# State update as a sum and a scaling, with transposes by the transpose operation, in a two-layer RWKV-7 and GLA backbone

## The chip, the core and the metric

The kernel runs on one core of a Trainium2 chip. The time is the device time of one execution in microseconds (us); of several runs the median is given. A core has five engines that run their own instruction streams and wait for each other by semaphores: TensorE (PE, with its weight loads shown as PEld), VectorE (DVE), ScalarE (ACT), GpSimd (POOL) and SyncE (SP, which issues the DMAs here).

## The reference, cut to what matters

Two layers over 512 latent and 256 context tokens of width 1024. Each has a token mixer (an input projection, an RWKV-7 branch and a GLA branch, both in two directions, gates, an output projection) and an MLP of width 4096, with normalisation and modulation around both. The change touches the recurrent states of the two branches:

```python
def rwkv7_scan(r, decay, k, v, kk, a, s0, reverse):
    def step(s, inp):
        r_t, w_t, k_t, v_t, kk_t, a_t = inp
        sa = jnp.einsum("bhvk,bhk->bhv", s, kk_t)
        s = (s * w_t[:, :, None, :]
             - sa[..., None] * (kk_t * a_t)[:, :, None, :]
             + v_t[..., None] * k_t[:, :, None, :])
        return s, jnp.einsum("bhvk,bhk->bhv", s, r_t)

def gla_chunked(q, k, v, log_alpha, s0):   # chunks of 64
    ...
    def step(s, inp):
        dec, kv = inp
        return s * dec[..., None] + kv, s
```

## The kernel before, in words

Activations are held with channels on the partitions and tokens along the free dimension. Large products (tiles `d`, from activations `sh`, `sl` and weights `wh`, `wl`) are made of three fp32r products of high and low parts; products of the recurrences are plain fp32 and take two passes on PE each.

The RWKV recurrence is done in chunks of 64 tokens. A unit is a pair of heads (p, 4 of them) and a group (gi, 3 of them: the context, then two halves of the latents) in both directions, so a layer has 12 RWKV units; 6 GLA units follow. For a unit, `rw_A1` and `rw_A2` make decays and scaled keys, `rw_B` makes masked products, transposes them (`pe.transpose`, tile `TK`) and inverts a triangular matrix, and `rw_C` walks four steps (chunks) in order. One step of `rw_C` (line 1335) multiplies the state `ZS` into `c` (line 1345), copies it to `pre` by ACT and DVE, multiplies by the inverse `YI`, copies to `ZA`, and updates the state: the product of `TK` and `ZA` (line 1364) is scaled by the chunk's decay `E` and added to the old state, which ACT has scaled by `E` into `zse` (line 1342). Per step that is four ACT copies and four DVE operations of 64x64, one for each of two directions and two heads (halves of the partitions). The last step of the last group needs no update, so a pair has 11 updating steps and a layer 44.

`gla_C` does the same with states `GZ` of 64x128 and the scaled copies `ze` (lines 1603 to 1609); its products `c<-GZ,KT` read only parts of `GZ` that are not the state, and are made for two steps at once. A layer has 22 such steps.

Row vectors on partitions become broadcast tiles by a product with the identity: `rstd_b` (line 812, tile `sc`), `sum_sq` (line 842, `rn`), the modulation vectors `da<-C,acc` (lines 764 and 1964). `C` holds the identity.

The order of the work is set by class `Order`. It records every instruction, gives each a price (`add`, line 209), and places them engine by engine in a list schedule: among those that can start first, the one of least `prio`, that is its place in the program, later by `LATE` for dense products (line 560). It issues them at one line, 566, which every row of the profile therefore has. Neighbouring PE products of one kind make one piece of the schedule (line 277). The mixer's program order comes from weaving threads per unit window: `nfill` and `nada` (line 103) say how many gate column blocks and modulation pieces each window gets, and `SEG` (line 142) gives the schedule's settings for the five flushed segments: the start, mixer, MLP, mixer, MLP.

Of the kernel before, what the change touches and what calls it, by code (L numbers as in the profile page):

```python
# [53 lines left out]
def constants():  # L54
# [45 lines left out]
SB = 6  # L100

CFG = {
    "nfill": ((2, 2, 0, 3, 1, 0, 3, 1, 0, 2, 2, 0, 2, 1, 1, 0, 0, 0, 0), (2, 3, 0, 2, 2, 1, 2, 2, 0, 2, 0, 0, 2, 1, 1, 0, 0, 0, 0)),
    "nada": ((2, 2, 2, 2, 2, 2, 2, 2, 2, 1, 2, 2, 0, 1, 0, 0, 0, 0, 0), (2, 1, 3, 1, 3, 2, 3, 1, 0, 0, 0, 0, 0, 0, 0, 0, 0, 0, 0)),
# [37 lines left out]
SEG = [  # L142
    dict(AHEAD=20.0, HOLD=8000.0, HYST=0.0, LATE=80000.0, LATEF=80000.0, SLACK=0.0, WARM=0.45),
    dict(AHEAD=100.0, HOLD=1000000000.0, HYST=0.0, LATE=20000.0, LATEF=20000.0, SLACK=0.0, WARM=0.45),
    dict(AHEAD=20.0, HOLD=1000000000.0, HYST=0.0, LATE=20000.0, LATEF=20000.0, SLACK=0.0, WARM=0.45),
    dict(AHEAD=20.0, HOLD=8000.0, HYST=0.0, LATE=20000.0, LATEF=20000.0, SLACK=0.0, WARM=0.45),
    dict(AHEAD=20.0, HOLD=1000000000.0, HYST=0.0, LATE=20000.0, LATEF=20000.0, SLACK=0.0, WARM=0.6),
]


class Order:
# [57 lines left out]
    def add(self, key, op, fn, a, k):  # L209
# [36 lines left out]
        else:  # L246
            c = max(w(out), max([w(x) for x in ins if x.ap and len(x.ap) > 1], default=0))
            onchip = [x for x in ins if hasattr(x.tensor, "cap_key")]
            if key == "ACT":
                n["d"] = 175.0 + 0.87 * c + (100.0 if any(isinstance(k.get(x), bass.AP) for x in ("bias", "scale")) and c > 64 else 0.0)  # L250
                n["table"] = 1 if k.get("func") == AF.Ln else 0 if k.get("func") in (AF.Exp, AF.Tanh) else None
            elif key == "POOL":
                if op == "memset":
                    n["d"] = 90.0 + 0.85 * c
                elif op in ("tensor_copy", "tensor_scalar"):
                    n["d"] = 180.0 + 0.87 * c
                elif k.get("op") == ALU.pow:
                    n["d"] = 380.0 + 160.0 * c
                else:
                    n["d"] = 185.0 + 2.16 * c  # L260
                n["two"] = op == "tensor_tensor"
            else:
# [6 lines left out]
                else:  # L269
                    n["d"] = 150.0 + 1.05 * c  # L270
        if key == "PE":
# [5 lines left out]
            if GROUP and p is not None and p.get("kind") == n["kind"] and p["calls"] < (3 if lhs.dtype == F32R else 4 if n["dense"] else 16):  # L277
# [51 lines left out]
    def flush(self):  # L329
# [6 lines left out]
        for n in ns:  # L336
# [6 lines left out]
            for name, t in ts.items():  # L343
                left[name] = left.get(name, 0) + 1
                if name not in self.serial:
                    key = t.cap_key
                    kk = self.slots.setdefault(key, {"cap": t.bufs or t.tag_meta.bufs, "free": [], "used": 0, "next": {}, "n": {}, "t0": self.free0})
                    sub = "da" if name.startswith("da_") else ""
# [225 lines left out]
def hybrid_kernel(ctx: ExitStack, tc: tile.TileContext, A: dict, out: bass.AP):  # L574
# [171 lines left out]
    def ada_steps(l, b0, pl, tag, bufs):  # L746
# [16 lines left out]
        for s in range(4):  # L763
            mm(pt[:, s].rearrange("p g r -> p (g r)"), acc[:, 128 * s:128 * s + 128], ident)
# [43 lines left out]
    def rstd_b(rb, streams, ps_pool, use):  # L808
        for s, o, n in streams:
            b = ps_pool.tile([P, 512], F32, name="d", tag="d")  # L810
            for t in range(o // 128, (o + n) // 128):
                mm(b[:, 128 * t - o:128 * t - o + 128], rb[:, 128 * t:128 * t + 128], ident)
            use(s, o, n, b[:, 0:n])

    def sum_sq(pl, xs, grp, cuts, eng=pool, psp=ops):
# [25 lines left out]
        for t in range(nt):  # L841
            mm(b[:, 128 * t:128 * t + 128], rn[:, t:t + 1].to_broadcast([P, 128]), ident)
# [81 lines left out]
    def mixer(l, acts, adas, pre, early):  # L924
# [399 lines left out]
        def rw_C(X, gi):  # L1324
# [10 lines left out]
            for st in range(4):  # L1335
                cc = (st, 7 - st)
                sl = slice(st, 8 - st, 7 - 2 * st)
                if not (gi == NG - 1 and st == 3):
                    zse = G([P, 2, 64], "zse", 1)
                    for d in range(2):  # L1340
                        for h in range(2):
                            act.activation(out=zse[HS[h], d], in_=zs[HS[h], cc[d], h, :], func=AF.Copy, scale=E[HS[h], cc[d]:cc[d] + 1])
# [15 lines left out]
                if st < 3:  # L1358
                    nz, ns = zs, (st + 1, 6 - st)
                else:  # L1360
                    nz, ns = nzs, (0, 7)
# [217 lines left out]
        def gla_C(X, gi):  # L1579
# [9 lines left out]
            for st in range(4):  # L1589
# [11 lines left out]
                cc = (st, 7 - st)  # L1601
                nz, ns = (z, (st + 1, 6 - st)) if st < 3 else (nz_, (0, 7))
                ze = G([P, 2, 128], "Q", 2, name="ze")
                for d in range(2):
# [470 lines left out]
```

## Time and profile before

| | us |
|---|---|
| median of 3 runs | 2871.23 |
| lowest and highest | 2870.66, 2878.29 |
| profiled execution | 2886.5 |
| its span | 2884.7 |
| PE busy | 2714.0 (94%) |
| DVE busy | 1603.8 (56%) |
| ACT busy | 1470.5 (51%) |
| POOL busy | 1172.0 (41%) |
| mean granted clock of PE | 0.967 |

The profile is of one execution, so its parts add up to its own 2886.5 us. PE's rows overlap each other, since a product's latency is counted with it: what a product takes is read from one start to the next. Tiles are named by the program; a row like `c<-ZA,TK` is an instruction that writes a tile `c` and reads `ZA` and `TK`.

### The profile page before, as it was taken

The numbers are of one execution on the slowest core, as the hardware profiler recorded it, in microseconds if no ns is written. First come the engines' busy times: TensorE is split into PE (matmuls) and PEld (weight loads), VectorE is DVE, ScalarE is ACT, GpSimd is POOL, SyncE is SP. The second block draws the span as 40 slices with busy tenths as digits, with TensorE's granted clock in tenths as the row PEclk, the third lists the DMA queues.
The fourth block names the chain that finished last, engine by engine and source line by source line (L and its number), as shares of the span: only waits on it lengthen the run. The fifth ranks groups of instructions, "written<-read, shape, count | busy, mean of one in ns | idle before, by whom it ended". The sixth has DMA issues, their size and how long they took to land.

```text
span 2884.7 us, 57083 instructions
## 1 busy us (share of the span) xinstructions
PE 2714.0 (94%) x22596; PEld 2249.0 (78%) x22596; DVE 1603.8 (56%) x3154; ACT 1470.5 (51%) x3144; POOL 1172.0 (41%) x1336
## 2 busy tenths in 40 slices
PE   7999999999989989999999899989988988999998
PEld 6777877788767878888888666767776766888887
DVE  6677787775576351122224547787877677622224
ACT  4565655666773452313134545656566785633333
POOL 3653444443321642313135546434434232733335
PEclk9999999999999999999998999999988999999999
DMA  6322333222226322222223342223211125433334
GB/s 232 110 85 73 97 95 97 84 90 65 87 94 229 94 77 63 64 64 64 63 70 116 119 143 87 77 85 90 92 34 35 34 77 182 136 106 97 97 95 136
DMA packets 148444, 276.59 MB, mean 96 GB/s; under 512 B 16496, under 2 KB 25456, under 8 KB 148176
## 3 DMA queue, kind: packets, MB, share of 16 engines
q1 hardware_dynamic: 148176, 272.93, 30.4%
q8 instruction: 178, 2.92, 0.4%
q14 instruction: 90, 0.74, 0.1%
HBM read 242.85 MB, written 30.02 MB: 95 GB/s over the span
## 4 chain that ended last, share of the span: by engine, by line
PE 51%; DVE 7%; ACT 4%; POOL 4%; issue 2%; DMA 1%; SPq 0%; POOLq 0%; ACTq 0%; DVEq 0%
PE d L566 43%; PE c L566 3%; PE m L566 2%; PE i L566 2%; POOL wl L566 1%; POOL S L566 1%; POOL x L566 1%; DVE sl L566 1%; DVE ZS L566 1%; DVE AR L566 1%; DVE u L566 1%; ACT zse L566 1%; PE da L566 1%; DVE GZ L566 0%; ACT f L566 0%
## 5 line engine op out<-in xcount | busy, mean ns | idle before, releaser
L566 PE MATMUL d<-sh,wh 128*128 128x512 f32 (+1 forms) x3280 | 1199.2, 366 | 39.0 <-ACT sh L566 13.2
L566 PE MATMUL d<-sh,wl 128*128 128x512 f32 (+1 forms) x3280 | 1142.4, 348 | 19.1 <-POOL wl L566 16.4
L566 PE MATMUL d<-sl,wh 128*128 128x512 f32 (+1 forms) x3280 | 1142.1, 348 | 4.4 <-DVE sl L566 3.0
L566 POOL TENSOR_TENSOR wl<-wr,wh 128x512 fp32r<-128x512 f32 x356 | 476.0, 1339 | 793.9 <-ACT wh L566 770.6
L566 PEld LDWEIGHTS d<-sh,wh 128*128 128x128 f32 x3280 | 631.3, 192 | 150.0 <-issue 36.5
L566 PEld LDWEIGHTS d<-sh,wl 128*128 128x128 f32 x3280 | 631.0, 192 | 103.8 <-POOL wl L566 21.9
L566 PEld LDWEIGHTS d<-sl,wh 128*128 128x128 f32 x3280 | 632.7, 193 | 69.0 <-DVE sl L566 5.4
L566 ACT ACTIVATE wh<-wr 128x512 fp32r<-128x512 f32 x580 | 361.9, 627 | 469.3 <-PE d L566 389.6
L566 DVE TENSOR_TENSOR wl<-wr,wh 128x512 fp32r<-128x512 f32 x224 | 171.5, 770 | 187.0 <-ACT wh L566 178.9
L566 DVE TENSOR_TENSOR t<-t,d 128x512 f32<-128x512 f32 (+1 forms) x101 | 58.2, 576 | 318.2 <-ACT t L566 318.1
L566 POOL TENSOR_TENSOR sl<-t,sh 128x512 fp32r<-128x512 f32 (+2 forms) x72 | 103.3, 1435 | 204.8 <-ACT sh L566 204.7
L566 DVE TENSOR_TENSOR a<-a,d 128x512 f32<-128x512 f32 (+1 forms) x80 | 44.3, 554 | 232.7 <-PE d L566 232.7
L566 ACT ACTIVATE zse<-ZS,E 64x64 f32<-64x64 f32 x352 | 121.3, 345 | 67.2 <-DVE ZS L566 62.7
L566 ACT ACTIVATE XY<-i 128x512 f16<-128x512 f32 x192 | 107.8, 591 | 59.1 <-PE i L566 57.1
L566 ACT ACTIVATE t<-d 128x512 f32<-128x512 f32 (+1 forms) x101 | 51.4, 509 | 161.4 <-PE d L566 161.3
L566 DVE SCALAR_TENSOR_TENSOR ZS<-c,E,zse 64x64 f32<-64x64 f32 x352 | 99.5, 283 | 34.6 <-PE c L566 27.6
L566 POOL TENSOR_TENSOR LTL<-AB,LTB 64x512 f16<-64x512 f32 x48 | 63.9, 1332 | 122.1 <-DVE LTB L566 88.1
L566 POOL TENSOR_TENSOR rn<-rn,C 128x2 f32<-128x2 f32 (+2 forms) x41 | 59.3, 1446 | 101.4 <-DVE rn L566 94.9
L566 POOL TENSOR_TENSOR S<-S,q 128x256 f32<-128x256 f32 x92 | 76.5, 838 | 56.5 <-ACT q L566 52.8
L566 PEld LDWEIGHTS <-XY 64*64 64x64 f16 x1920 | 65.7, 110 | 38.9 <-issue 27.2
L566 DVE TENSOR_TENSOR Q<-i,MK 128x512 f16<-128x512 f32 x120 | 82.7, 689 | 23.3 <-PE i L566 20.7
L566 ACT ACTIVATE f<-d 128x512 f32<-128x512 f32 (+1 forms) x85 | 54.0, 644 | 79.1 <-PE d L566 69.2
(255 smaller groups left out, 4309.6 us busy)
## 6 DMA issues: line engine op xcount, KB each, us to landing
wr<-in_w_dram SPq DMA_DIRECT2D x304, 256.0 KB, 2.6
wr<-in_win_dram SPq DMA_DIRECT2D x180, 256.0 KB, 2.9
wa<-in_ada_dram SPq DMA_DIRECT2D x160, 256.0 KB, 2.7
wr<-in_wmrg_dram SPq DMA_DIRECT2D x64, 256.0 KB, 2.9
ra<-in_ada_dram SPq DMA_DIRECT2D x32, 256.0 KB, 5.4
wr<-in_wout_dram SPq DMA_DIRECT2D x32, 256.0 KB, 3.0
gdr<-fg SPq DMA_DIRECT2D x20, 384.0 KB, 2.9
gdr<-fg SPq DMA_DIRECT2D x20, 256.0 KB, 2.3
```

What stands on the lines that cost most here:

```text
L566: ins = fn(*a, **k).ins
```

## The change

The state update becomes one sum and one scaling: (product + old state) times decay. In layer one the sum is a DVE addition into a scratch tile `gs` with one buffer, then a DVE multiplication by `E` broadcast along the free dimension; both take the two directions in one operation, so there are two additions and two multiplications of 64x128 per step. In layer two (`ACCUM`) PE adds the old state in PSUM by a product of the identity with `ZS`, and only the two multiplications are left to DVE. The GLA steps of both layers use the form with the addition, at 64x256, with a scratch tile `gs2` of two buffers. The products with the identity named above become `pe.transpose`. Prices, settings and the tables of the schedule change with it.

```diff
+ACCUM = (False, True)
...
-    "nfill": ((2, 2, 0, 3, 1, 0, 3, 1, 0, 2, 2, 0, 2, 1, 1, 0, 0, 0, 0), (2, 3, 0, 2, 2, 1, 2, 2, 0, 2, 0, 0, 2, 1, 1, 0, 0, 0, 0)),
+    "nfill": ((2, 2, 0, 2, 2, 0, 2, 2, 0, 2, 2, 0, 2, 1, 1, 0, 0, 0, 0), (2, 3, 0, 2, 2, 1, 2, 2, 0, 2, 2, 0, 1, 0, 0, 1, 0, 0, 0)),
...
+SEG = [dict(LATE=1e6, LATEF=1e6), dict(LATE=20e3, LATEF=20e3), {}, {}, {}]
...
-                n["d"] = 175.0 + 0.87 * c + (100.0 if any(isinstance(k.get(x), bass.AP) for x in ("bias", "scale")) and c > 64 else 0.0)
+                n["d"] = 175.0 + 0.87 * c + (110.0 if any(isinstance(k.get(x), bass.AP) for x in ("bias", "scale")) and c > 32 else 0.0)
...
-                    n["d"] = 185.0 + 2.16 * c
+                    n["d"] = 215.0 + 2.25 * c
...
-                    n["d"] = 150.0 + 1.05 * c
+                    n["d"] = 150.0 + 1.05 * c + (60.0 if op == "scalar_tensor_tensor" and isinstance(k.get("scalar"), bass.AP) else 0.0)
...
-            mm(pt[:, s].rearrange("p g r -> p (g r)"), acc[:, 128 * s:128 * s + 128], ident)
+            pe.transpose(pt[:, s].rearrange("p g r -> p (g r)"), acc[:, 128 * s:128 * s + 128], ident)
...
-                mm(b[:, 128 * t - o:128 * t - o + 128], rb[:, 128 * t:128 * t + 128], ident)
+                pe.transpose(b[:, 128 * t - o:128 * t - o + 128], rb[:, 128 * t:128 * t + 128], ident)
...
-            mm(b[:, 128 * t:128 * t + 128], rn[:, t:t + 1].to_broadcast([P, 128]), ident)
+            pe.transpose(b[:, 128 * t:128 * t + 128], rn[:, t:t + 1].to_broadcast([P, 128]), ident)
...
-                if not (gi == NG - 1 and st == 3):
-                    zse = G([P, 2, 64], "zse", 1)
-                    for d in range(2):
-                        for h in range(2):
-                            act.activation(out=zse[HS[h], d], in_=zs[HS[h], cc[d], h, :], func=AF.Copy, scale=E[HS[h], cc[d]:cc[d] + 1])
...
                 for d in range(2):
-                    mm(fl(pr[:, d]), tk[:, cc[d]], fl(za[:, cc[d]]))
-                for d in range(2):
-                    for h in range(2):
-                        hs = HS[h]
-                        dve.scalar_tensor_tensor(out=nz[hs, ns[d], h, :], in0=pr[hs, d, h], scalar=E[hs, cc[d]:cc[d] + 1],
-                                                 in1=zse[hs, d], op0=ALU.mult, op1=ALU.add)
+                    if ACCUM[l]:
+                        mm(fl(pr[:, d]), ident, fl(zs[:, cc[d]]), stop=False)
+                    mm(fl(pr[:, d]), tk[:, cc[d]], fl(za[:, cc[d]]), start=not ACCUM[l])
+                for h in range(2):
+                    hs = HS[h]
+                    src = pr[hs, :, h]
+                    if not ACCUM[l]:
+                        src = G([P, 2, 64], "gs", 1)[hs]
+                        dve.tensor_tensor(out=src, in0=pr[hs, :, h], in1=zs[hs, sl, h, :], op=ALU.add)
+                    dve.tensor_tensor(out=nz[hs, ns, h, :], in0=src, in1=E[hs, sl].unsqueeze(2).to_broadcast([64, 2, 64]), op=ALU.mult)
...
-                ze = G([P, 2, 128], "Q", 2, name="ze")
-                for d in range(2):
-                    for h in range(2):
-                        hs = HS[h]
-                        act.activation(out=ze[hs, d], in_=z[hs, cc[d], h, :], func=AF.Copy, scale=E[hs, cc[d]:cc[d] + 1])
-                        dve.scalar_tensor_tensor(out=nz[hs, ns[d], h, :], in0=pu[hs, st % 2, d], scalar=E[hs, cc[d]:cc[d] + 1],
-                                                 in1=ze[hs, d], op0=ALU.mult, op1=ALU.add)
+                gs = G([P, 2, 128], "Q", 2, name="gs2")
+                for h in range(2):
+                    hs = HS[h]
+                    dve.tensor_tensor(out=gs[hs], in0=pu[hs, st % 2], in1=z[hs, sl, h, :], op=ALU.add)
+                    dve.tensor_tensor(out=nz[hs, ns, h, :], in0=gs[hs], in1=E[hs, sl].unsqueeze(2).to_broadcast([64, 2, 128]), op=ALU.mult)
```

`nada` becomes two pieces for each of the first 12 windows of layer one and the first 8 of layer two, with the same totals; `SEG` loses its limits on how far ahead DMAs are issued (HOLD) in the first and fourth segment.

The order that follows differs in both mixers from end to end. Three places show what the update becomes. On ACT, in a unit window of layer two, the row of `zse` stood in front of the copy `pre` before:

```order
L566 ACTIVATE XY<-i 128x512 x2
L566 ACTIVATE zse<-ZS,E 64x64 x4
L566 ACTIVATE pre<-c 64x128
L566 ACTIVATE ZS<-VT 64x4x64
L566 ACTIVATE wh<-wr 128x512
```

and now ACT has in such a place (`XY` and `Q` are of the inverse, `E`, `Ep`, `lw` decays of a later unit):

```order
L561 ACTIVATE XY<-i 128x512 x2
L561 ACTIVATE pre<-c 64x128
L561 ACTIVATE E<-lw 128x3
L561 ACTIVATE Ep<-lw,C 128x260
L561 ACTIVATE ZA<-c 64x2x64
```

Nothing that scales the state stands between the inverse's copies and `pre` any more. On PE, a step's update product in layer two, before (`LTB` is of the inverse):

```order
L566 MATMUL d<-sh,wl 128x512
L566 MATMUL c<-ZA,TK 128x128 x2
L566 MATMUL da<-wa,SC 32x128 x4
L566 MATMUL c<-ZS,AR 128x128 x2
L566 LDWEIGHTS LTB
```

and now:

```order
L561 MATMUL d<-sh,wl 128x512
L561 MATMUL c<-ZS,C 128x128
L561 MATMUL c<-ZA,TK 128x128
L561 MATMUL c<-ZS,C 128x128
L561 MATMUL c<-ZA,TK 128x128
L561 LDWEIGHTS LTB
```

One product with the identity stands before the first product that reads `ZA`, the other behind it. On DVE, in the GLA windows of layer two, before:

```order
L566 SCALAR_TENSOR_TENSOR GZ<-c,E,ze 64x128 x4
L566 SCALAR_TENSOR_TENSOR sc<-f,PR,sc 128x769 x2
L566 SCALAR_TENSOR_TENSOR GZ<-c,E,ze 64x128 x4
L566 TENSOR_TENSOR sl<-bon,sh 128x512
L566 SCALAR_TENSOR_TENSOR GZ<-c,E,ze 64x128 x4
```

and now, each multiplication reading what the addition in front of it wrote:

```order
L561 TENSOR_TENSOR gs_20341<-c,GZ 64x256
L561 TENSOR_TENSOR GZ<-gs_20341,E 64x2x128
L561 TENSOR_TENSOR gs_20341<-c,GZ 64x256
L561 TENSOR_TENSOR GZ<-gs_20341,E 64x2x128
L561 SCALAR_TENSOR_TENSOR y<-y,PR,d 128x512
```

Where four independent operations stood, two dependent pairs stand.

## Rows read from the trace of the kernel before

**Rows 1.** The page: the span, and the granted clock in 40 slices (tenths)

```profile
span 2884.7 us, 57083 instructions
...
PEclk9999999999999999999998999999988999999999
...
```

**Rows 2.** Windows: length, busy us and count of PE, PEld, DVE, ACT, POOL; clock, DMA

```profile
...
124.00:719.00 595.00, 583.24 (x6867) 473.96 (x6868) 440.21 (x936) 356.25 (x838) 259.25 (x334) 1.00 0.28 85
719.00:873.00 154.00, 139.68 (x1144) 112.24 (x1138) 103.91 (x220) 111.89 (x227) 39.27 (x58) 0.96 0.28 90
1029.00:1550.00 521.00, 517.88 (x2918) 451.83 (x2917) 116.90 (x199) 157.21 (x281) 162.06 (x123) 1.00 0.23 68
1746.00:2270.00 524.00, 483.14 (x5646) 383.57 (x5644) 405.01 (x854) 322.41 (x771) 227.50 (x289) 0.93 0.23 68
2270.00:2410.00 140.00, 116.89 (x912) 90.42 (x911) 100.24 (x201) 107.39 (x222) 35.81 (x60) 0.93 0.22 68
...
```

**Rows 3.** Chain of waits, shares of the windows 1746:2270 and 2270:2410

```profile
...
by line: PE d L566 26.9%; PE c L566 17.4%; PE i L566 8.8%; PE m L566 8.3%; DVE ZS L566 3.7%; issue 3.5%; ACT zse L566 3.3%; DVE AR L566 3.0%; PE da L566 2.7%; DVE ZA L566 2.0%; DVE AB L566 1.8%; DVE YI L566 1.1%; DVE Q L566 1.0%; DVE pre L5
...
by line: issue 20.6%; PE d L566 14.7%; DVE GZ L566 9.5%; DVE lw L566 5.8%; DVE sc L566 5.3%; ACT L566 4.6%; DVE QS L566 4.4%; PE m L566 4.2%; ACT ta L566 3.4%; PE c L566 3.3%; ACT ze L566 2.8%; ACT GZ L566 2.4%; ACT f L566 2.1%; ACT sc L566
...
```

**Rows 4.** Timeline, one step of layer two: start us, us, engine, line, operation, count [idle]

```profile
...
2123.99 1.20 DVE L566 SCALAR_TENSOR_TENSOR ZS<-c,E,zse 64x64 f32<-64x64 f32 x4
...
2124.96 0.77 PE L566 MATMUL c<-ZS,AR 128*128 128x128 f32 x4
...
2125.22 1.42 ACT L566 ACTIVATE zse<-ZS,E 64x64 f32<-64x64 f32 x4 [0.89 <-DVE ZS L566]
...
2126.66 0.27 ACT L566 ACTIVATE pre<-c 64x128 f32<-64x128 f32 x1
...
```

**Rows 5.** Groups by form: busy us, mean ns of one, idle before

```profile
...
L566 ACT ACTIVATE zse<-ZS,E 64x64 f32<-64x64 f32 x352 | 121.3, 345 | 67.2 <-DVE ZS L566 62.7
...
L566 DVE SCALAR_TENSOR_TENSOR ZS<-c,E,zse 64x64 f32<-64x64 f32 x352 | 99.5, 283 | 34.6 <-PE c L566 27.6
...
L566 ACT ACTIVATE ze<-GZ,E 64x128 f32<-64x128 f32 x176 | 70.0, 398 | 11.6 <-DVE GZ L566 7.7
...
L566 DVE SCALAR_TENSOR_TENSOR GZ<-c,E,ze 64x128 f32<-64x128 f32 x176 | 61.5, 349 | 10.6 <-PE c L566 5.1 <-ACT ze L566 0.4
...
L566 DVE TENSOR_TENSOR acc<-acc,da 128x128 f32<-128x128 f32 x140 | 39.0, 283 | 32.7 <-PE da L566 30.4
...
L566 DVE TENSOR_TENSOR BK<-ta,Ep 64x256 f32<-64x256 f32 x48 | 30.9, 644 | 1.4
...
L566 PE MATMUL d<-C,sc 128*128 128x128 f32 x176 | 26.0, 294 | 1.1 <-ACT sc L566 1.1
...
L566 DVE TENSOR_TENSOR AR<-r,lw 64x256 f32<-64x256 f32 x40 | 19.9, 498 | 0.2
...
L566 DVE TENSOR_TENSOR QS<-m,MK 64x256 f32<-64x256 f32 x40 | 16.9, 422 | 11.6 <-PE m L566 11.0
...
L566 PE MATMUL d<-C,rn 128*128 128x128 f32 x84 | 16.0, 324 | 6.0 <-DVE u L566 3.1 <-POOL rn L566 2.7
...
L566 PE MATMUL da<-C,acc 128*128 128x128 f32 x48 | 7.4, 287 | 0.8 <-ACT acc L566 0.8
...
```

**Rows 6.** Timeline of PE: four transposes, four products with the identity, the next

```profile
...
487.38 0.63 PE L566 MATMUL m<-C,BK 128*128 128x128 f32 x4
487.84 1.06 PE L566 MATMUL da<-C,acc 128*128 128x128 f32 x8
488.73 0.56 PE L566 MATMUL c<-pre,YI 128*128 128x64 f32 x4
...
```

**Rows 7.** Timeline, DVE in layer two's GLA: a dependent pair, and four updates

```profile
...
2330.54 0.42 DVE L566 TENSOR_TENSOR lw<-lw,ta 128x256 f32<-128x256 f32 x1 [4.51 <-ACT ta L566]
...
2331.06 0.70 DVE L566 TENSOR_TENSOR_SCAN lw<-C,lw 128x260 f32<-128x260 f32 x1
...
2339.00 1.50 DVE L566 SCALAR_TENSOR_TENSOR GZ<-c,E,ze 64x128 f32<-64x128 f32 x4
...
```

More of the change, by code (lines that the diff above doesn't have):

```diff
@@ L100 @@
 SB = 6
+ACCUM = (False, True)
 CFG = {
-    "nfill": ((2, 2, 0, 3, 1, 0, 3, 1, 0, 2, 2, 0, 2, 1, 1, 0, 0, 0, 0), (2, 3, 0, 2, 2, 1, 2, 2, 0, 2, 0, 0, 2, 1, 1, 0, 0, 0, 0)),
-    "nada": ((2, 2, 2, 2, 2, 2, 2, 2, 2, 1, 2, 2, 0, 1, 0, 0, 0, 0, 0), (2, 1, 3, 1, 3, 2, 3, 1, 0, 0, 0, 0, 0, 0, 0, 0, 0, 0, 0)),
+    "nfill": ((2, 2, 0, 2, 2, 0, 2, 2, 0, 2, 2, 0, 2, 1, 1, 0, 0, 0, 0), (2, 3, 0, 2, 2, 1, 2, 2, 0, 2, 2, 0, 1, 0, 0, 1, 0, 0, 0)),
+    "nada": ((2,) * 12 + (0,) * 7, (2,) * 8 + (0,) * 11),
     "nout": ((3, 2, 2), (2, 2, 1)),
@@ L141 @@
 HYST = 0.0
[L142 to L148, printed above, removed]
+SEG = [dict(LATE=1e6, LATEF=1e6), dict(LATE=20e3, LATEF=20e3), {}, {}, {}]
 class Order:
@@ L276, in add @@
             p = self.nodes[-1] if self.nodes else None
-            if GROUP and p is not None and p.get("kind") == n["kind"] and p["calls"] < (3 if lhs.dtype == F32R else 4 if n["dense"] else 16):
+            if GROUP and p is not None and p.get("kind") == n["kind"] and p["calls"] < (3 if lhs.dtype == F32R else 8 if n["dense"] else 16):
                 p["call"].append((fn, a, k))
@@ L347, in flush @@
                     kk = self.slots.setdefault(key, {"cap": t.bufs or t.tag_meta.bufs, "free": [], "used": 0, "next": {}, "n": {}, "t0": self.free0})
-                    sub = "da" if name.startswith("da_") else ""
+                    sub = "da" if name.startswith(("da_", "wa_")) else ""
                     k = kk["n"].setdefault(sub, 0)
@@ L1358, in rw_C @@
                 if st < 3:
[L1359 removed]
+                    nz, ns = zs, slice(st + 1, 7 - st, 5 - 2 * st)
                 else:
[L1361 removed]
+                    nz, ns = nzs, slice(0, 8, 7)
                 pr = cps.tile([P, 2, 2, 64], F32, name="c", tag="c")
                 for d in range(2):
[L1364 to L1369 removed]
+                    if ACCUM[l]:
[8 more added lines that the diff above has]
+                    dve.tensor_tensor(out=nz[hs, ns, h, :], in0=src, in1=E[hs, sl].unsqueeze(2).to_broadcast([64, 2, 64]), op=ALU.mult)
                 yield
@@ L1600, in gla_C @@
                             mm(pu[64:128, s2, d], kt[0:64, 4 * d + c, 64:128], z[0:64, 4 * d + c, 1])
-                cc = (st, 7 - st)
-                nz, ns = (z, (st + 1, 6 - st)) if st < 3 else (nz_, (0, 7))
-                ze = G([P, 2, 128], "Q", 2, name="ze")
-                for d in range(2):
-                    for h in range(2):
-                        hs = HS[h]
-                        act.activation(out=ze[hs, d], in_=z[hs, cc[d], h, :], func=AF.Copy, scale=E[hs, cc[d]:cc[d] + 1])
-                        dve.scalar_tensor_tensor(out=nz[hs, ns[d], h, :], in0=pu[hs, st % 2, d], scalar=E[hs, cc[d]:cc[d] + 1],
-                                                 in1=ze[hs, d], op0=ALU.mult, op1=ALU.add)
+                sl = slice(st, 8 - st, 7 - 2 * st)
+                nz, ns = (z, slice(st + 1, 7 - st, 5 - 2 * st)) if st < 3 else (nz_, slice(0, 8, 7))
+                gs = G([P, 2, 128], "Q", 2, name="gs2")
[3 more added lines that the diff above has]
+                    dve.tensor_tensor(out=nz[hs, ns, h, :], in0=gs[hs], in1=E[hs, sl].unsqueeze(2).to_broadcast([64, 2, 128]), op=ALU.mult)
                 yield
@@ L1963, in hybrid_kernel @@
             pt = cps.tile([P, 4, 4, 32], F32, name="da", tag="c")[:, 0]
-            mm(pt.rearrange("p g r -> p (g r)"), au, ident)
+            pe.transpose(pt.rearrange("p g r -> p (g r)"), au, ident)
             dve.tensor_tensor(
```

## The prediction

> **What bounds the kernel now.** I read the page first: the span is 2884.7 us, and three of the 40 slices of the granted clock (the 22nd, 30th and 31st) stand at 8, the others at 9 [rows 1]: TensorE loses clock at the start and late in layer two's mixer. Then the table by stage [rows 2], where five stretches answer most. In the MLP (1029 to 1550) PE is busy 517.88 of 521 us at full clock: columns bound it, and the change leaves its products alone. In layer one's RWKV stretch PE is busy 583.24 of 595 at clock 1.00: bound by PE too. In layer two's RWKV stretch PE is busy 483.14 of 524 at clock 0.93, DVE 405.01: here PE waits 41 us, and 7% of the stretch's columns are lost to the low clock (37 us). Both GLA stretches (719 to 873, 2270 to 2410) are loose: PE idles 14 and 23 us, DVE is busy 67% and 72%. Together the four mixing stretches leave 11.8 + 14.3 + 40.9 + 23.1 = 90 us of PE idle, and by the clock column 6 + 37 + 10 = 53 us: that is all that faster chains or a better order could take out of them.
>
> Third, the chain of waits [rows 3]. In layer two's RWKV stretch ACT's scaled copies (zse) make 3.3% of the path, 17.3 us, and DVE's state updates (ZS) 3.7%, 19.4 us. In layer two's GLA stretch DVE's updates (GZ) are 9.5% of 140 us, 13.3 us, and ze 2.8%, 3.9 us. How the first comes about shows in one step [rows 4]: four updates end at 2125.19, four zse follow until 2126.64, and the copy `pre` on ACT starts at 2126.66, although the product it reads (c<-ZS,AR, 2124.96 for 0.77 us) was done at 2125.73. The scaled copies are queued in front of it.
>
> **The change, part by part.** Counts: zse runs 352 times in fours, so there are 88 RWKV steps, 44 a layer; ze 176 times, so 44 GLA steps, 22 a layer [rows 5].
>
> *TensorE.* Four transposes start at 487.38 and the next group at 487.84: 0.115 us each. Four fp32 products with the identity, each two passes, take from 487.84 to 488.73: 0.2225 us each [rows 6]. A converted product saves 0.108 us. The rows count passes, so d<-C,sc x176, d<-C,rn x84 and da<-C,acc x48 are 88, 42 and 24 products [rows 5]: 154 x 0.108 = 16.6 us saved. Layer two gains 88 identity products (two a step): 88 x 0.2225 = 19.6 us. PE's net work is +3 us: on that account alone nothing happens.
>
> *RWKV steps of layer two.* All zse go: 17.3 us of the path. Two DVE multiplies replace four updates. Nearest row for a 64x128 operation that reads PSUM: 283 ns (acc<-acc,da, also 128 elements wide), against 283 ns for each old update [rows 5]: four to two halves 19.4 us, -9.7. Of the two identity products the first stands in front of the product that waits for ZA, so PE makes it in that wait; the second stands behind it and is on the path: 44 x 0.2225 = +9.8. Transposes (40 for norms, 8 for adaLN): -5.2. Sum -22.4. But PE is the next late: it is busy 92% of the stretch, and work that the chain uncovers waits for it. I take a little over half, -13. Bounds: -32 if both identity products hide; +14 if both are on the path and everything else of the chain is refilled.
>
> *RWKV steps of layer one.* A step's DVE work becomes add, multiply, add, multiply, strictly one after another, because the scratch tile has one buffer. An add is 283 ns. For a multiply from SBUF alone at 64x128 no row exists; from below it is the 283 ns, from above half way into the 64x256 rows of that kind, 498 to 644 ns [rows 5]; I take 330. A dependent pair leaves 0.10 us between (2330.54 + 0.42 = 2330.96, next 2331.06) [rows 7]. So 2 x (0.283 + 0.330) + 3 x 0.10 = 1.53 us against 1.20 us for four updates [rows 4]: +0.33 x 44 = +14 us of DVE, which goes from 440 to 454 of 595, hidden under PE (583 of 595). 60 us of zse leave ACT, hidden as well. What counts in a stretch bound by PE is its 48 + 12 transposes: -6.5 us. Bounds -6.5 and +8, if DVE's 14 us are not hidden.
>
> *GLA steps.* An add 64x256 from PSUM is 422 ns, a multiply 498 to 644, nearest the middle, 530 [rows 5]. 2 x (0.422 + 0.530) + 3 x 0.10 = 2.2 us against 1.50 us for four updates [rows 7]: +0.7 x 22 = +15.4 us of DVE a layer. ACT loses 88 x 0.398 = 35 us a layer. On the path: 13.3 x 2.2 / 1.5 - 13.3 = +6.2, less the 3.9 of ze: +2.3 a layer, +5 in all. Bounds: -8 (ze goes, the updates hide) and +31 (all of DVE's growth is paid).
>
> [...]
>
> *Transposes outside the mixers* (42 for norms, 4 at the start): -5.0 us, in stretches where PE partly waits for others; -3. Bounds -5 and 0.
>
> *The order drawn anew.* The list scheduler's prices change, so both mixers are reordered; the MLPs nearly keep theirs. Before, it priced a zse at 175 + 0.87 x 64 = 231 ns and an update at 150 + 1.05 x 64 = 217; the rows say 345 and 283 [rows 5]. A step's eight instructions were priced 0.72 us too short, and what was placed behind them came late. Those two are gone, and their successors are priced right (150 + 1.05 x 128 = 284 for the 283). Against it: gate blocks of layer two move forward, away from its late RWKV windows, which thins the dense columns there. I take -8; bounds -35 and +35, a quarter of the 143 us of idle and lost clock, either way.
>
> Sum: -13 - 6.5 + 5 - 3 - 8 = -25.5 us. The profiled execution took 2886.5 us (1.8 around its span), so 2861; the runs' median, 2871.2, lies 15 us under the profiled one, and there it makes **2846 us**.
>
> **Rivals.**
> *PE binds everywhere.* Its work changes by +3 us, and whatever DVE and ACT give back is refilled with its waits. For it: 92 to 98% busy in the RWKV stretches. Against it: 41 us of idle in layer two. 2871, within 8.
> *DVE becomes the bound of the GLA stretches: slower.* Each step's pairs are serial on DVE. It goes from 104 to 119 of 154 us and from 100 to 116 of 140; it decides once DVE's instructions end most of PE's and ACT's waits there. Price +31, in place of the +5, and no gain from the order: -13 - 6.5 + 31 - 3 = +8.5 with layer one's DVE work hidden, -13 + 8 + 31 - 3 = +23 with it paid. Between them, about 2886. Against it: ACT is 33 to 35 us lighter there, and ACT was the busier engine of the two.
> *The new order closes far more idle.* With -35 and the chain's full -22: 2871 - 35 - 22 - 6 + 5 - 3 = 2810. For it: 143 us are there. Against it: the new settings let DMA issues run further ahead in layer two, and nothing in the rows says that weights came late there.
> *The new order is worse*, by its +35: 2889, from thinner dense work in layer two's late windows, where the clock is already low.
> *The transposes cost the clock.* Layer one at layer two's 0.93 would lose 7% of 595, 42 us: 2846 + 42 = 2888. Against it: that stretch already holds groups of transposes at clock 1.00 [rows 2, 6]. [...]
>
> **How the numbers follow.** Forecast 0.44 (its own range 2822 to 2860), PE binds 0.17, DVE binds GLA 0.15, large gain from the order 0.14, worse order 0.06, clock 0.04. A change under 0.3% (8.6 us) can't be told from none here. Faster: 0.42 of the forecast, the 0.14, and 0.03 of the PE case: 0.59. Slower: 0.14 of the DVE case, 0.06, 0.04, and 0.02 of the PE case: 0.26. The rest, 0.15, is the same. The range, 2800 to 2893, takes in the large gain and the three slow cases, and leaves some 2 in 10 beyond for orders better or worse than their bounds.
>
> **What the profile after would show.** ACT has no zse or ze, and `pre` starts when its product ends; the chain of layer two's RWKV stretch has no zse and half of ZS. Identity products c<-ZS,C x176 passes, PE idle there under 41 us. Transposes appear as 154 single passes. In GLA DVE's share rises to 77% and 83%; if the stretches are longer than 154 and 140 us, the DVE rival is right. If layer two's RWKV stretch is not shorter than 524 us, my main term is wrong; if layer one's differs from 595 by over 10 us, the order did it, not the transposes.

## The result: slower by half a per cent

The changed kernel takes 2890.97 us (median of 5 runs, 2885.74 to 2895.27) against 2876.61 us for the kernel before beside it: ratio 1.0056, interval [1.0038, 1.0075]. Forecast were 2846 us and "faster". Measured once more beside other kernels it was 2888.98 against 2878.69: 1.0036 [1.0022, 1.0050]. So it is 10 to 14 us slower, where I expected 25 less.

The page of the changed kernel's profiled execution (2890.97 us with 1.8 around its span): span, busy time with shares and instructions by engine, and the granted clock in 40 slices. It answers to [rows 1].

```profile
span 2889.2 us, 56492 instructions
...
PE 2718.2 (94%) x22618; PEld 2253.3 (78%) x22618; DVE 1627.2 (56%) x3066; ACT 1285.0 (44%) x2616; POOL 1179.0 (41%) x1336
...
PEclk9999999999999889999999899999978989999999
...
```

ACT lost its scaled copies (1285 us busy), PE's busy time hardly moved, and six slices of the clock are under 9 where three were; two of them (the 14th and 15th, 939 to 1083 us) lie between layer one's GLA and its MLP, where none did. Of the three before, the 22nd (1514 to 1587 us, at 0.88) is the end of layer one's MLP and what follows it; at the start, where I read lost clock, 1.00 was granted (0 to 124 us). The stretches of [rows 2], moved to where they now lie (columns as there):

```profile
...
125.00:716.00 591.00, 574.59 (x6823) 468.38 (x6824) 456.30 (x943) 294.38 (x656) 256.52 (x332) 1.00 0.28 86
716.00:870.00 154.00, 140.02 (x1085) 112.80 (x1082) 116.57 (x208) 79.76 (x141) 42.92 (x58) 0.94 0.27 86
1033.00:1554.00 521.00, 515.86 (x2883) 450.82 (x2884) 113.85 (x191) 151.88 (x269) 157.04 (x119) 0.98 0.22 67
1754.00:2275.00 521.00, 482.57 (x5738) 389.24 (x5736) 378.57 (x765) 261.06 (x592) 222.60 (x283) 0.94 0.22 65
2275.00:2410.00 135.00, 114.29 (x877) 88.76 (x876) 106.29 (x196) 73.25 (x135) 40.73 (x61) 0.90 0.22 67
...
```

Layer one's RWKV stretch went from 595 to 591 us, the MLP stayed at 521, layer two's RWKV stretch went from 524 to 521, its GLA from 140 to 135. The second row keeps the length that it had before; cut at instructions, as in the table below, layer one's GLA is 158.1 us long, where it was 154.0. PE idles 38.4 us in layer two's RWKV stretch (40.9 before) though ACT is busy 261 us there, not 322. The chain of waits in the last two stretches, by line, beside [rows 3]:

```profile
...
by line: PE d L561 29.8%; PE c L561 21.9%; PE i L561 11.2%; PE m L561 10.3%; DVE AR L561 3.5%; PE da L561 3.0%; issue 1.7%; DVE BK L561 1.2%; DVE lw L561 1.2%; DVE ZA L561 1.1%; DVE YI L561 1.1%; DVE XO L561 0.9%; DVE AB L561 0.9%; DVE ZS L
...
by line: issue 25.3%; PE d L561 15.1%; PE m L561 9.6%; DVE lw L561 8.1%; DVE sc L561 5.7%; PE c L561 5.5%; DVE GZ L561 3.7%; DVE gs L561 3.1%; DVE QS L561 3.1%; ACT f L561 2.1%; ACT sc L561 1.9%; ACT ta L561 1.9%; DVE sl L561 1.8%; POOL KI 
...
```

In layer two's RWKV stretch zse is gone and ZS, 3.7% before, stands under 1%. But the four largest PE rows (d, c, i, m) rose from 61.4% of 524 us to 73.2% of 521, from 322 to 381 us of the path: what left the chain PE took over. In GLA the additions and multiplications together are 6.8% of 135 us, 9.2 us, where GZ and ze were 12.3% of 140, 17.2 us. One step, beside [rows 4]:

```profile
...
2087.64 0.27 ACT L561 ACTIVATE ZA<-c 64x128 f32<-64x128 f32 x1 [1.37 <-PE c L561]
...
2088.35 0.39 PE L561 MATMUL d<-sh,wl 128*128 128x512 f32 x1
...
2088.58 0.38 PE L561 MATMUL c<-ZS,C 128*128 128x128 f32 x2
...
2088.80 0.39 PE L561 MATMUL c<-ZA,TK 128*128 128x128 f32 x2
...
2089.02 0.39 PE L561 MATMUL c<-ZS,C 128*128 128x128 f32 x2
...
2089.24 0.39 PE L561 MATMUL c<-ZA,TK 128*128 128x128 f32 x2
...
2090.05 0.59 DVE L561 TENSOR_TENSOR ZS<-c,E 64x128 f32<-64x128 f32 x2
...
2091.45 0.61 PE L561 MATMUL c<-ZS,AR 128*128 128x128 f32 x4
...
2092.14 0.26 ACT L561 ACTIVATE pre<-c 64x128 f32<-64x128 f32 x1
...
```

Product after product the two identity products (c<-ZS,C, each two passes) and the two with ZA come at 0.22 us each. In this step the first is not made in the wait for ZA: ZA on ACT starts at 2087.64 and takes 0.27, and PE makes dense products (d) until 2088.58. DVE's two multiplications end at 2090.64, `pre` starts on ACT at 2092.14, right behind its product (2091.45 + 0.61): no copy stands in front of it. The groups by form, beside [rows 5]:

```profile
...
L561 DVE TENSOR_TENSOR ZS<-gs,E 64x128 f32<-64x128 f32 x88 | 44.5, 506 | 3.0
L561 DVE TENSOR_TENSOR GZ<-gs,E 64x256 f32<-64x256 f32 x88 | 43.7, 497 | 2.9
...
L561 PE MATMUL c<-ZS,C 128*128 128x128 f32 x176 | 39.0, 306 | 0.0
...
L561 DVE TENSOR_TENSOR gs<-c,GZ 64x256 f32<-64x256 f32 x88 | 37.0, 420 | 13.9 <-PE c L561 12.6
...
L561 DVE TENSOR_TENSOR gs<-c,ZS 64x128 f32<-64x128 f32 x88 | 25.2, 287 | 13.1 <-PE c L561 10.9
L561 DVE TENSOR_TENSOR ZS<-c,E 64x128 f32<-64x128 f32 x88 | 25.2, 286 | 17.6 <-PE c L561 16.5
...
L561 PE MATMUL d<-C,sc 128*128 128x128 f32 x88 | 14.8, 296 | 0.2 <-ACT sc L561 0.2
...
L561 PE MATMUL d<-C,rn 128*128 128x128 f32 x42 | 10.9, 352 | 11.4 <-DVE u L561 7.4 <-POOL rn L561 3.8
...
```

Transposes appear as 88 (d<-C,sc) and 42 (d<-C,rn) single passes; with 24 of da they are the 154.

**Where the time lies.** I cut each span at the starts of the same instructions: RWKV from a layer's first product c<-ZS,AR to its first c<-GZ,KT, GLA from there to its last c<-GZ,QS, "norm" from there to the ninth t<-t,d of the MLP, the MLP from there to the first d<-C,rn behind it. The last two rows are of experiments below: the changed operations with the settings of before, and the changed kernel with one price raised by 1 ns.

| us | start | RWKV 1 | GLA 1 | norm | MLP 1 | to RWKV 2 | RWKV 2 | GLA 2 | rest | span |
|---|---|---|---|---|---|---|---|---|---|---|
| before | 123.8 | 595.1 | 154.0 | 198.3 | 478.6 | 195.9 | 535.8 | 127.1 | 476.0 | 2884.7 |
| changed | 124.8 | 591.1 | 158.1 | 201.4 | 478.6 | 199.6 | 533.4 | 122.3 | 480.0 | 2889.2 |
| old settings | 122.9 | 599.7 | 148.2 | 194.8 | 478.5 | 195.6 | 534.8 | 119.0 | 474.7 | 2868.2 |
| 1 ns | 124.7 | 596.4 | 150.9 | 193.3 | 478.6 | 203.7 | 520.7 | 116.2 | 478.5 | 2863.0 |

The profiled execution of before lay 10 us over its runs' median and that of the changed kernel on its own, so this pair of traces shows only 4.5 of the 14 us. The comparisons below go by the timed runs.

### The profile page after: what moved, and what is told of

Its sections match the earlier page's. It is cut to its first block, busy times and chain, and to the rows that moved or that the text cites. A ratio compares the mean times of both kernels' runs of the same rounds, so it can differ in the third digit from the quotient of the medians.

```text
span 2889.2 us, 56492 instructions
## 1 busy us (share of the span) xinstructions
PE 2718.2 (94%) x22618; PEld 2253.3 (78%) x22618; DVE 1627.2 (56%) x3066; ACT 1285.0 (44%) x2616; POOL 1179.0 (41%) x1336
## 5 line engine op out<-in xcount | busy, mean ns | idle before, releaser
L561 PE MATMUL i<-Q,XY 64*64 64x64 f16 x1920 | 83.2, 198 | 11.8 <-DVE Q L561 9.1
L561 PEld LDWEIGHTS <-LTB 128*128 128x128 f16 x1344 | 62.3, 100 | 24.4 <-issue 19.6
```

Source lines behind the costliest of these rows:

```text
L561: ins = fn(*a, **k).ins
```

## The experiments

Each was timed in five rounds against the kernel before on the same chip. "Operations" are the state updates and the transposes; "settings" are the tables `nfill` and `nada`, `SEG`, and the scheduler's prices with two more that the section on the change leaves out: the most dense products in one piece (8, 4 before) and a ring of their own for the `wa` tiles.

**1. Which half of the change costs?** t_same: the transposes alone, priced so that every engine keeps the order of before.

```diff
-            mm(b[:, 128 * t:128 * t + 128], rn[:, t:t + 1].to_broadcast([P, 128]), ident)
+            pe.transpose(b[:, 128 * t:128 * t + 128], rn[:, t:t + 1].to_broadcast([P, 128]), ident)
...
+            if op == "transpose" and n["w"][0][0].name.startswith("d"):
+                op = "matmul"
```

> The kernel before with the transposes alone, in exactly its order (they are priced as the products they replace). If a transpose saves what its spacing says, 154 x 0.108 = 16.6 us of PE; of it the part in stretches bound by PE counts: 7 to 17 us faster, ratio 0.994 to 0.998. If transposes cost the clock, the low clock in the normalisation stretches (about 960 to 1060 us) grows and the time is the same or up to 15 us longer.

2871.78 us, ratio 0.9979 [0.9970, 0.9989]: -6 us. Layer one's RWKV stretch takes 599.0 us (595.1): the 42 us that the clock was to lose there did not come. A smaller loss did: with every engine in the same order, the granted clock is 0.9652 in the mean of this version's 12 runs (0.963 to 0.968) and 0.9697 in that of the 27 of before beside them (0.966 to 0.973). At some 2 us for 0.001, the slope within both kernels' runs (last section), that is an estimated 9 us; at equal clock the transposes would be worth some 14. The traces do not show where the clock fell, since both profiled executions had 0.967.

s_only: the state updates alone, at the old settings, with products for the transposes.

```diff
+                    if ACCUM[l]:
+                        mm(fl(pr[:, d]), ident, fl(zs[:, cc[d]]), stop=False)
...
+                    dve.tensor_tensor(out=nz[hs, ns, h, :], in0=src, in1=E[hs, sl].unsqueeze(2).to_broadcast([64, 2, 64]), op=ALU.mult)
```

> The new state updates (RWKV and GLA) alone, with the old prices, tables and settings, and products with the identity where the new kernel has transposes; the order is drawn anew. If DVE's serial pairs in the GLA stretches cost what the rival said: +10 to +30 us, and both GLA stretches longer than 154 and 140 us. If the shorter chain of layer two wins: 5 to 20 us faster, with its RWKV stretch under 524 us.

2872.84 us, 0.9985 [0.9972, 0.9998]: -4 us. GLA takes 151.5 and 123.0 us, not longer but shorter than 154.0 and 127.1.

st: both, at the old settings.

```diff
 # the two edits above together; nfill, nada, SEG and prices as before
```

> State updates and transposes, with the old prices, tables and settings. If the settings made the loss: faster than before by the 10 to 25 us that the settings alone cost less, so 2850 to 2865 us. If the operations did it: 2885 to 2900 us, like the whole change.

2865.43 us, 0.9960 [0.9945, 0.9976]: -11.5 us, about the sum of the two. Faster than both kernels. Here the order is drawn anew, and the transposes cost no clock: 0.972 in the mean of the runs, 0.971 in those of s_only.

c_only: the new settings with the operations of before.

```diff
+SEG = [dict(LATE=1e6, LATEF=1e6), dict(LATE=20e3, LATEF=20e3), {}, {}, {}]
...
+                    n["d"] = 215.0 + 2.25 * c
```

> The operations of the kernel before, with the new prices, tables and settings of the schedule alone. If the settings are what made the kernel slower: +10 to +25 us, ratio 1.004 to 1.009. If the new operations did it: within 6 us of before; if the better prices help and the operations cost more than the whole loss: 5 to 15 us faster.

2888.68 us, 1.0046 [1.0032, 1.0061]: +13 us, at a granted clock of 0.962 in the mean of its runs against 0.970: at the same 2 us for 0.001 the clock alone is more than the excess. So the operations gain at the old settings, and the excess comes with the settings, with the orders that they draw. At the changed settings this one pair shows no gain of the operations: 1.0046 without them, 1.0056 and 1.0036 with them.

**2. Which setting?** The version st with one part of the settings each, and the changed kernel with the old SEG.

```diff
 # st_tables: st, with
+    "nada": ((2,) * 12 + (0,) * 7, (2,) * 8 + (0,) * 11),
 # st_seg: st, with
+SEG = [dict(LATE=1e6, LATEF=1e6), dict(LATE=20e3, LATEF=20e3), {}, {}, {}]
 # st_prices: st, with
+                n["d"] = 175.0 + 0.87 * c + (110.0 if any(isinstance(k.get(x), bass.AP) for x in ("bias", "scale")) and c > 32 else 0.0)
 # after_oldseg: the changed kernel, with
+    dict(AHEAD=20.0, HOLD=8000.0, HYST=0.0, LATE=80000.0, LATEF=80000.0, SLACK=0.0, WARM=0.45),
```

> The version with the new operations and the old settings, plus the two new tables (nfill, nada) alone; prices and SEG as before. Theory 'tables': the new spread of adaLN pieces and dense blocks over the windows thins the end of layer one's mixer and layer two's late RWKV windows, and it carries most of the +26 us that lie between the two full versions: ratio to the kernel before about 1.003 (0.996 without it), with the norm stretch between layer one's GLA and the MLP some 5 us longer and over 31 us at the low clock there. Rivals 'SEG' and 'prices': this version stays at 0.996 +- 0.002. Rival 'no single part': about a third of the way, 0.999.

> The version with the new operations and the old settings, plus the new SEG alone (how early transfers are issued and how late pieces may be placed); prices and tables as before. Theory 'tables' or 'prices': 0.996 +- 0.002, no difference from the version without it. Rival 'SEG': it carries most of the 26 us, ratio about 1.003, and the new waits end on transfers. Rival 'no single part': 0.999.

> The version with the new operations and the old settings, plus the new prices of ACT and DVE, groups of 8 dense products where 4 stood, and the ring for wa_ (these set which instruction the scheduler puts next); tables and SEG as before. Rival 'prices': the prices are nearer to the measured durations and still draw the worse order; ratio about 1.003, layer two's two mixing stretches longer by 10 us or more. Theory 'tables': 0.996 +- 0.002. My prediction's step (prices that fit the rows make a better order) would have it under 0.996. Rival 'no single part': 0.999.

> The changed kernel with the SEG of before, all else as changed. Theory 'tables' or 'prices': no difference from the changed kernel, ratio to the kernel before 1.0056 +- 0.002. Rival 'SEG': most of the 26 us come back, 0.997 to 0.999. Rival 'no single part': 1.002.

Measured: st_tables 2879.16 us, 1.0008 [0.9997, 1.0019]; st_seg 2877.84 us, 1.0004 [0.9988, 1.0020]; st_prices 2873.14 us, 0.9993 [0.9978, 1.0008]; after_oldseg 2870.58 us, 0.9977 [0.9964, 0.9990]. Each part alone costs 9 to 14 us on st, 36 together; all three cost 25, and tables with prices (after_oldseg) only 5. No theory of one guilty part fits parts that don't add up. That the time depends on which of many orders the scheduler lands on fits them, and this was tried next.

**3. Is it the setting, or the draw?** The general price of a DVE instruction, in the scheduler alone, raised by 1 ns: a number without meaning, which reorders the program from layer one's mixer on. (In the changed kernel the line goes on with its term for `scalar_tensor_tensor`.)

```diff
-                    n["d"] = 150.0 + 1.05 * c
+                    n["d"] = 151.0 + 1.05 * c
```

> The changed kernel with the general price of a DVE instruction raised by 1 ns (151 where 150 stood): the same operations, tables and settings, and a number that means nothing, which yet draws the list schedule anew from layer one's mixer on. Theory 'draw' (every new order is a draw with a scatter of some 10 us, and the changed kernel's is a bad one): the time moves by 5 us or more from the changed kernel's 1.0056, most likely down, to 0.997 to 1.003. Rival 'settings' (tables, SEG and prices are worse in themselves): 1.0056 +- 0.002.

> The version with the new operations and the old settings, with the same 1 ns on DVE's general price. Theory 'draw': the 0.996 was a good draw, and this one moves up by 5 us or more, to 0.998 to 1.002. Rival 'settings': the old settings are better in themselves, 0.996 +- 0.002.

The changed kernel with 151 takes 2867.79 us, 0.9961 [0.9949, 0.9974], 0.85% or 24 us under the mean of its two ratios with 150; st goes to 2865.19 us, 0.9946 [0.9926, 0.9966]. The rival "settings" as I had put it (1.0056 +- 0.002) falls for the changed kernel. For st it came out as it said (0.996 +- 0.002), and my "draw", up by 5 us or more, did not. Two windows each, first of the changed kernel, then of the version with 151: the end of layer one's GLA with most of the norm stretch (from the 160th c<-GZ,QS to the fourth t<-t,d), and layer two's RWKV stretch (columns as in [rows 2]).

```profile
...
862.00:1057.00 195.00, 176.13 (x944) 151.78 (x941) 109.26 (x190) 78.68 (x161) 78.60 (x76) 0.88 0.40 135
1754.00:2287.00 533.00, 493.39 (x5838) 398.03 (x5838) 382.82 (x769) 268.10 (x603) 226.76 (x290) 0.95 0.21 64
...
```

```profile
...
860.00:1047.00 187.00, 170.02 (x941) 145.39 (x938) 107.08 (x190) 79.48 (x162) 77.39 (x76) 0.92 0.41 140
1748.00:2268.00 520.00, 480.43 (x5798) 388.45 (x5799) 382.03 (x769) 265.87 (x597) 224.82 (x289) 0.96 0.21 65
...
```

In layer two 533 us against 520, at equal PE idle (39.6 us in both): all 13 us are PE's busy time, 493.4 against 480.4. With more digits the granted clock is 0.946 against 0.961, which is 29.0 against 20.5 us lost; the other 4 us are work that the version with 151 makes ahead of this stretch and behind it (12 dense and 16 small products by the records). In the norm window 195 against 187: 6 us of busy time at 0.88 against 0.92, and 2 us of idle. GLA makes another 13. Over the whole spans 104.5 against 80.6 us are lost to the clock, 24 of the 26 us between these two executions. But the same order profiled once more (after_again, 2886.9 us) lost 92.7 us and idled 177.8 where 151 idles 161.4: there it is 12 us of clock and 16 of waits, less some of work, out of 24. So an order sets both, in shares that change from one execution to the next.

after_hold: the changed kernel with the limit on how far ahead transfers are issued put back, because I had named it against the gain from the order.

```diff
+SEG = [dict(LATE=1e6, LATEF=1e6, HOLD=8e3), dict(LATE=20e3, LATEF=20e3, HOLD=1e9), {}, dict(HOLD=8e3), dict(HOLD=1e9)]
```

> The changed kernel with the limit on how far ahead transfers are issued (HOLD = 8 us) put back in the start and in layer two's mixer; of SEG only LATE of the start, AHEAD of layer one's mixer and WARM of the last MLP stay as changed. Theory 'HOLD' (transfers issued too far ahead in layer two collide with others): the 23 us that the whole old SEG gave come back here too, 0.998, and they come back in layer two's stretches. Rival 'LATE': no change, 1.0056 +- 0.002. Theory 'draw': anything from 0.997 to 1.006, with the stretches of layer one, before which only the start was touched, moved as much as those of layer two.

2879.36 us, 1.0002 [0.9986, 1.0017]: some 13 us back in the ratio to the changed kernel's mean, where the whole old SEG gave 20; layer two's RWKV stretch stays at 533.7 us, and the gain lies before it. That is no sign of HOLD in layer two; one more order between the others.

**4. How wide are the draws, and what is left when they are averaged?** The changed kernel once more, and the 1 ns steps for all three versions.

```diff
 # after_149, before_149, st_149 (after_152 has 152.0, before_151 has 151.0)
+                    n["d"] = 149.0 + 1.05 * c
```

> The changed kernel itself, unaltered, once more beside the nudged orders. Theory 'draw' (the excess belongs to this one order): 1.0056 +- 0.002, and 20 us or more above after_149 or the earlier 1 ns version. Rival (the chip or the hour made it): 0.996 to 0.999.

> The changed kernel with DVE's general price lowered by 1 ns (149). Theory 'draw': anywhere from 0.994 to 1.006, most likely 0.999, the mean of the nine versions with the new operations so far (0.9946 to 1.0056). Rival 'the changed prices are a bad region and 151 was the lucky one': 1.004 to 1.007.

> The kernel before with DVE's general price raised by 1 ns (151): its operations, tables and settings, another order. Theory 'draw': it moves by 3 us or more; about 1.002, with 0.995 to 1.009 possible. Rival 'the order of before is a good one among its draws': 1.004 to 1.010, since every other order is worse. Rival 'orders matter little': 1.000 +- 0.0015.

> The kernel before with DVE's general price lowered by 1 ns (149). The same three expectations as for 151: about 1.002 (0.995 to 1.009), 1.004 to 1.010, or 1.000 +- 0.0015. If the operations are worth the 11 us that one pair at equal settings showed, the mean of before's orders lies some 0.004 above the mean of the changed kernel's.

> The version with the new operations and the old settings, DVE's general price lowered by 1 ns (149). Theory 'the operations are worth some 0.4% at the old settings, whatever the draw': 0.993 to 0.999, under the 1.0016 of the kernel before at the same price. Rival 'they are worth nothing, 0.996 and 0.9946 were two good draws': 1.000 +- 0.004, above 0.999 more likely than not.

> The changed kernel with DVE's general price raised by 2 ns (152). Theory 'draw, with settings that are worth nothing in themselves': 0.994 to 1.003, most likely 0.998, under the changed kernel's 1.0046. Rival 'the changed settings are worse in themselves': 1.002 to 1.007, with 0.9961 at 151 the exception.

| DVE's price | before | operations alone (st) | changed kernel |
|---|---|---|---|
| 149 | 1.0016 [1.0004, 1.0028] | 0.9961 [0.9946, 0.9976] | 1.0000 [0.9988, 1.0013] |
| 150 | 1 | 0.9960 [0.9945, 0.9976] | 1.0056 and 1.0036, mean 1.0046 |
| 151 | 0.9978 [0.9966, 0.9989] | 0.9946 [0.9926, 0.9966] | 0.9961 [0.9949, 0.9974] |
| 152 | | | 1.0024 [1.0015, 1.0033] |
| mean | 0.9998 | 0.9956 | 1.0008 |

The excess belongs to the order: the same order measured again (after_again, 2888.98 us) has the same stretches (RWKV 2 531.8 us, norm 201.4, GLA 157.8 and 120.6) and nearly the same time, and its neighbours lie up to 0.85% below. Three things come out. At the old settings the operations are worth 0.3 to 0.55% at each price, 0.42% or 12 us in the mean; before's own three draws scatter by 0.2%, so this is uncertain by some 3 us. The settings cost 0.15 to 0.86% at each price, in the mean of all draws 0.52%, 15 us; with four draws from 0.9961 to 1.0046 this size is uncertain by some 5 us (their scatter over the root of four). And the changed kernel's own draw lies 0.38%, 11 us, above the mean of its family. -12 + 15 + 11 = +14. The parts are differences of the table's means, so that they add up is no further test; the measured +10 to +14 is what they split.

**5. Does the product with the identity pay?** st_ff: st with layer two's sum made by DVE, as in layer one.

```diff
-ACCUM = (False, True)
+ACCUM = (False, False)
```

> The version with the new operations and the old settings, with layer two's sum made by DVE as in layer one (ACCUM = False, False): 88 identity products fewer on PE (19.6 us by 0.2225 us each), 88 additions of 64x128 more on DVE. My terms: one of two products a step on the path (-9.8 us of PE), and the additions +0.38 us a step pair on the chain, 44 x 2 x 0.38 = +33 us at most and about half of it at the share I took: +7 us, 0.998 to 1.000. Rival 'PE binds layer two as well': the 19.6 us come out, 0.989. Theory 'draw': the sign can't be read from one order; within +-10 us of 0.996.

2898.32 us, 1.0069 [1.0048, 1.0091]: 31 us above st, where the draws of one version lie at most 24 us apart, and those of st 4 us; but it is one order too. Layer two's RWKV stretch of st, its GLA stretch, and then that RWKV stretch of st_ff:

```profile
...
1740.00:2275.00 535.00, 494.22 (x5863) 399.48 (x5864) 388.98 (x774) 268.15 (x603) 227.61 (x291) 0.94 0.21 66
2275.00:2394.00 119.00, 98.03 (x780) 75.39 (x776) 102.20 (x192) 66.01 (x123) 35.65 (x54) 0.94 0.23 72
...
```

```profile
...
1734.00:2301.00 567.00, 498.50 (x5671) 392.64 (x5668) 420.60 (x862) 267.89 (x604) 227.26 (x292) 0.90 0.20 62
...
```

567 us against 535, at clock 0.90 against 0.94. PE idles 68.5 us, not 40.8, though it makes 88 products fewer. The groups of st_ff:

```profile
...
L567 DVE TENSOR_TENSOR ZS<-gs,E 64x128 f32<-64x128 f32 x176 | 83.4, 474 | 5.9
...
L567 DVE TENSOR_TENSOR gs<-c,ZS 64x128 f32<-64x128 f32 x176 | 50.6, 287 | 28.4 <-PE c L567 24.2
...
```

A step in layer two gets two additions of 0.287 us on its chain: 44 x 2 x 0.287 = 25 us, which, with the slower multiplications, is about the 28 us by which PE's idle grew. The clock adds to it: PE's busy time is 4 us longer with 19.6 us less of work, because 54.6 us are lost to the clock in the stretch, not 30.7. The products cost PE less than the chain and the clock paid for the additions.

## Why the prediction was wrong

**The failing step: "The order drawn anew", -8.** I argued that prices nearer to the durations would place instructions better. The runs say otherwise: the prices alone cost some 9 us on st (one draw), and settings and draw together made +26 of it, by the split above. The bounds, +-35, held that; the value had the wrong sign, and the chances were wrong in putting only 0.06 on a worse order. The rival's place was half right: against the neighbour with 151 the changed kernel loses 13 us in layer two's RWKV stretch, 8.5 of them to a lower clock, as the rival had it, but also 8 in the norm stretch and 13 in GLA, which I had not named, and wins 9 back in RWKV 1 and ahead of RWKV 2. Why one order is worse than another, no run shows; what they show is that on st neither prices nearer to the durations nor another part of the settings made it better. A step that can't be worked out from rows, and whose bounds are wider than the rest of the sum, should have carried the sign's uncertainty: without it my sum was -17.5, with it anything from -52 to +18.

**RWKV of layer two, -13: it gave nothing.** -2 in the pair of traces; over the three orders of st against the three of before +1.6 (531.8 against 530.2). My own test, "not shorter than 524 us", it passed by 3 us, which is within the draws. I had written that work which the chain uncovers waits for PE, and still took over half; the chain after shows PE's rows where zse and ZS were. Also, the first identity product, which I had put into the wait for ZA, stands behind it in the step shown. The rival "PE binds" was right here. What the chain is worth shows in the other direction: longer by 25 us (st_ff) it cost 33, the clock's part included.

**RWKV of layer one, -6.5:** -4 in the pair, -1.7 in the means (596.4 against 598.1). DVE rose to 456 us, hidden under PE (574.6 of 591 us) as said. That this meets the 454 worked out is luck: the multiplication took 506 ns, not 330 (+15 us in 88), and the 13 us of gaps between the four operations, which I had counted as busy, are not.

**GLA, +5: wrong sign at the old settings.** In the means of three orders each it went from 154.5 to 150.5 us and from 127.5 to 118.7: -13, the largest gain of the operations. At the changed settings layer one shows none of it: 155.1 us in the mean of four orders, where the one order of c_only has 146.7 (layer two: 119.4 and 120.0). The step's durations were right (0.420 + 0.497 against 0.422 + 0.530); what I undervalued is most likely ACT's 35 us a layer, of which I counted the 3.9 us that ze had on the chain: ACT was busier than DVE there before [rows 2], and in st it is busy 66 of 119 us. The time that DVE waited for ACT in the two stretches fell from 31 and 23 us to 18 and 8 in st. No run took ze away alone, so this stays argued. The DVE rival falls in size: DVE is busy 76% and 79% (77% and 83% worked out); in the pair of traces layer one's stretch is 4 us longer and layer two's 5 shorter, where the rival priced +31, and DVE ended 23 of the 74 us that ACT waited there and 11 of 50, not most.

**Transposes:** 6 us in t_same, against 5.2 + 6.5 + 3 = 14.7 in the sum. At equal clock they come to the estimated 14 us, so PE's work was counted rightly; what is missing is the clock, which fell from 0.9697 to 0.9652. The clock rival falls as I priced it, 42 us in layer one's RWKV stretch, but in the order of before it had a part, some 9 us, that my sum put at nothing. Why the clock fell in t_same, no run shows; in st, in its own order, it did not (0.972 against 0.971 in s_only).

## What to carry to other kernels

Where a scheduler sets the order from prices, one version's time is one draw: here 1 ns on one price moved it by up to 0.85%, more than the operations were worth (0.42%); the other two versions moved by 0.38% and 0.15%. So compare changes over several neighbouring orders, keep the best one, and give a redrawn order no expected gain, only a width. Put the granted clock of the runs beside their times: a saving of work can be real and be hidden by a lower clock, as in t_same (6 us of an estimated 14, at 0.9652 against 0.9697). In layer two's RWKV stretch, where PE is busy 92%, a shorter chain brought nothing here, while a longer one cost more than itself (33 us for 25); in the loose GLA stretches the same change gave more than its rows' share of the chain (13 us), at the old settings.

## What the runs showed of the hardware

Multiplications of DVE that read both operands from SBUF took longer beside GpSimd's operations, 46 of 176 in the changed kernel. The two operations of a layer-one step, from the changed kernel's view of one tile (ns: least, median, most):

```profile
...
L561 DVE TENSOR_TENSOR gs<-c,ZS x88: 256/286/298, 152.5 to 687.9; 64x128 f32<-64x128 f32 x88
L561 DVE TENSOR_TENSOR ZS<-gs,E x88: 282/290/1326, 152.8 to 688.3; 64x128 f32<-64x128 f32 x88
...
```

The medians agree, the longest is 1326 ns against 298. DVE's rows in one step, and then GpSimd's at that place:

```profile
...
218.53 0.28 DVE L561 TENSOR_TENSOR gs<-c,ZS 64x128 f32<-64x128 f32 x1 [0.30 <-PE c L561]
218.84 1.12 DVE L561 TENSOR_TENSOR ZS<-gs,E 64x128 f32<-64x128 f32 x1
...
220.19 0.30 DVE L561 TENSOR_TENSOR gs<-c,ZS 64x128 f32<-64x128 f32 x1
220.52 0.29 DVE L561 TENSOR_TENSOR ZS<-gs,E 64x128 f32<-64x128 f32 x1
...
```

```profile
...
218.78 1.04 POOL L561 TENSOR_TENSOR sc<-f 128x512 f32<-128x512 f32 x1
...
```

GpSimd's operation runs from 218.78 to 219.82; the multiplication that starts at 218.84 ends at 219.96, 0.14 us behind it, where the second one takes 0.29. Of the 176 multiplications from SBUF (ZS<-gs, GZ<-gs) 46 are long (over 350 and 480 ns); every one of them overlaps an operation of GpSimd and ends some 0.15 or 0.28 us after one, and without such an overlap none is longer than 291 and 424 ns. The additions and layer two's multiplications, with one operand in PSUM, show none (at most 298 ns for 64x128), though 52 of layer one's 88 additions overlap an operation of GpSimd. In one place, at 227.14 us, GpSimd's operation began 51 ns behind the multiplication, and this took 289 ns. So the mean is 506 where I took 330; PE, busy 574.6 of the stretch's 591 us, covered it. The same is in the rows of before from which I took the 498 to 644 ns of a 64x256 operation: without a GpSimd operation beside it none of them takes more than 427 ns, so that for a GLA step such rows give 2 x (0.422 + 0.427) + 3 x 0.10 = 2.0 us where GpSimd is not in the way, and not the 2.2 that I took. Why a multiplication takes longer there, the traces do not show.

Within one kernel a slower run is mostly a run at lower clock: fitted with one slope over the runs of a version and those of before beside it, the time falls by 1.5 to 2.4 us for 0.001 of the mean granted clock in all 18 comparisons, 2.0 in t_same's (the correlation r within one version's runs is from -0.55 to -0.93, but -0.14 in after_152, whose clocks lie within 0.003). Between kernels the mean clock does not rank them, since their work and waits differ: t_same had 0.965 in the mean of its runs and 2872 us, st_tables 0.971 and 2879 us. Taking that slope for the difference between two versions is an estimate.
